# A hybrid layer's FFN in two phases: second phase's operands in small steps, first weight block earlier, last group by column halves

## The chip, the cores and the metric

The kernel runs on one core of a Trainium2 chip. The metric is the device time of one execution in microseconds; the median of three runs of the kernel before is 2200.96 us (2199.82 to 2202.98). The engines are named as in the profile: PE multiplies matrices, PEld loads its weights, DVE, ACT and POOL work on elements, SP issues every DMA of this kernel in one ordered queue.

## The reference

One layer of a two-mixer trunk over 2048 positions and 1024 channels, all in float32: an S5 state-space mixer and an mLSTM mixer, joined by an output projection, then a feed-forward part (FFN) with a squared ReLU, and a last norm:

```
x = x + concat(S5, mLSTM) @ W_out
h = rmsnorm(x, norm_ffn_g)
x = x + square(relu(h @ W1)) @ W2        # 1024 -> 4096 -> 1024
return rmsnorm(x, final_norm_g)
```

The mixers are not touched by the change.

## The kernel before

**Layout.** Channels lie on the 128 partitions, positions along the free axis; a tile of 512 positions is a token block. Blocks 0 and 1 make the FFN's first phase, blocks 2 and 3 its second. Every large product is made of float16 high and low parts, three matmuls for one (L1300, L1301, L1302 in the FFN).

**Stages in time.** The mixers take the span to about 735 us, then come the gated unit of S5 (to 800), the output projection of blocks 0 and 1 (to 840), that of blocks 2 and 3 in alternation (to 935), FFN phase 1 of 2 (935 to about 1600), phase 2 (to 2176), and the last norm with the stores (to 2199.5).

**The FFN.** Both of its products go by a seven-product scheme on 2 x 2 blocks (Strassen-Winograd), so the operands are not the plain blocks but sums and differences of them, each split into a high and a low part. `f1_stream` runs over 16 units of W1 in each phase. A unit is seven products in two half steps each, and its results, after the ReLU and square, become seven pairs B11, B21, T2, T1, T3, B22, T4 in the tag "hd", a ring of 22 buffers of 2 KB per partition. `f2_stream` runs over 8 groups of W2 per phase, a group being four row pairs (mp) of seven products of 512 columns; each product is added to the accumulator `accx` by a DVE operation at L1399. The main loop takes one half step of F1 and one product of F2 in turn, F2 behind by LAG = 34.

**Operands of F1.** `hprep(ph, k, rb)` makes one quarter k of the seven operands: four norms on DVE (L1129, multiply by a gain and by the row factor `rb`, which lies in PSUM), four subtractions in `combos` (L1085 to L1094), seven splits (L1079: ACT copies the high part, L1080: POOL or DVE subtracts it, POOL in five of seven). For phase 1 the operands go into resident tiles `hop`. For phase 2 the block's x comes from a DRAM buffer `x2d` (L1128) into hd buffers, and each pair is stored to the DRAM buffer `hopd` (L1115), to be loaded when phase 2 begins. These four calls stand at i = 2, 6, 10 and 14 of the main loop, the first half steps of phase 1.

**Weights.** Each raw block of 1 MB is loaded (`w1_load` L1160, `w2_load` L1209), reduced to its largest value (L1148), scaled and split (L1178 ACT, L1179 DVE); POOL makes the weight sums (L1192, L1232 to L1235). `w2_load` has a single buffer, "stg"; W1's raw blocks alternate between "w0" and "w1". The first block of W1 is loaded, scaled and prepared between m = 3 and m = 5 of the output projection of blocks 2 and 3, beside `hprep(0, ...)`.

**Ends.** `final0` writes the output of phase 1 while phase 2 runs: for each of 16 tiles a load from the DRAM buffer `x2f`, a norm on DVE (L1439) and a store, every fourth i, all through the one buffer of tag "tb". `final1` does the same for phase 2 at the very end: row sums, row factors, then 10 multiplies on DVE (L1458), 6 on ACT and POOL (L1455, L1456), 8 stores of 512 KB (L1460).

**Order.** A scheduler at build time puts the instructions of each engine in a fixed order by its own cost estimates; on the chip each engine runs its list in that order and waits where an operand is late. SP does so too, so a DMA that waits for its buffer holds every DMA behind it.

## Time and profile before

| what | value |
|---|---|
| median of three runs | 2200.96 us |
| profiled execution, its time | 2201.49 us |
| its span | 2199.5 us |
| PE busy | 2045.9 us, 93% |
| DVE busy | 1702.6 us, 77% |
| ACT, POOL busy | 48%, 51% |

The profiled execution lies 0.5 us above the median, and its span leaves 2.0 us of its time outside. A row of a table by stretches gives start and end in us, the stretch's length, then for each engine its busy time in it with the number of instructions, the mean granted clock of PE (1 is 2.4 GHz, 0.5 is 1.2 GHz), the share of time that the DMA engines were busy and what they moved in GB/s. A busy PE is no PE at its peak, so the number of matmuls in a stretch says more than the busy time.

### The profile page before, as it was taken

What the parts mean: (1) busy time and instruction counts of PE and PEld (TensorE: products, weight loads), DVE (VectorE), ACT (ScalarE), POOL (GpSimd) and SP (SyncE); (2) the same over time, 40 slices, a digit from 0 to 9 for tenths busy, and PEclk for the clock granted to TensorE, in tenths of its full rate; (3) what the DMA queues carried; (4) which work ended last, traced back from release to release, by engine and by line L of the source; (5) the groups of instructions that cost most, each with busy time, mean ns of one, the idle gap of its engine ahead of it and who ended that gap; (6) DMA issues with size and microseconds to landing.
All of it is one profiled execution on the core that took longest, in us unless ns stands there. A gap on an engine that the chain in (4) does not pass through costs nothing.

```text
span 2199.5 us, 29564 instructions
## 1 busy us (share of the span) xinstructions
PE 2045.9 (93%) x11021; PEld 1148.6 (52%) x11021; DVE 1702.6 (77%) x2829; ACT 1055.5 (48%) x1879; POOL 1125.3 (51%) x1095
## 2 busy tenths in 40 slices
PE   6999899899998799867999999999999899999996
PEld 4987767676776344333444444444444344444442
DVE  7878888887867544978988888878887786777776
ACT  5426455555544222345545454545564354545443
POOL 2135566564223201567665655565684566557454
PEclk9999999999999899988999999999999999999998
DMA  5111111211103212343111111115332321111102
GB/s 174 60 52 57 50 44 30 82 34 54 63 20 134 87 39 71 116 149 125 58 58 58 58 58 58 58 58 191 134 134 101 134 72 58 58 48 68 39 20 96
DMA packets 53551, 168.14 MB, mean 76 GB/s; under 512 B 7776, under 2 KB 17184, under 8 KB 40864
## 3 DMA queue, kind: packets, MB, share of 16 engines
q1 hardware_dynamic: 53408, 166.26, 22.5%
q8 instruction: 86, 1.41, 0.3%
q14 instruction: 57, 0.47, 0.1%
HBM read 129.44 MB, written 28.41 MB: 72 GB/s over the span
## 4 chain that ended last, share of the span: by engine, by line
PE 56%; DVE 22%; DMA 7%; POOL 5%; ACT 3%; issue 3%; SPq 1%; POOLq 0%; DVEq 0%; ACTq 0%
PE gx L1300 4%; PE gx L1302 4%; PE gx L1301 4%; PE fx L1300 4%; PE fx L1301 4%; PE fx L1302 4%; PE gv L1300 2%; PE gv L1302 2%; PE gv L1301 2%; PE fv L1302 2%; PE fv L1300 2%; PE fv L1301 2%; PE po L157 2%; PE po L158 2%; PE po L159 2%
## 5 line engine op out<-in xcount | busy, mean ns | idle before, releaser
L1178 ACT ACTIVATE w2o<-r,fs_b 128x512 f16<-128x512 f32 (+1 forms) x128 | 105.4, 824 | 153.3 <-PE gx L1302 76.3
L1329 ACT ACTIVATE e<-e 128x512 f32<-128x512 f32 x96 | 60.3, 628 | 211.0 <-DVE e L1369 93.0
L1301 PEld LDWEIGHTS <-w2o 128*128 128x128 f16 x896 | 87.7, 98 | 128.3 <-issue 27.3
L1179 DVE SCALAR_TENSOR_TENSOR w2o<-r,fs_b,w2o 128x512 f16<-128x512 f32 (+1 forms) x128 | 132.9, 1039 | 25.7 <-ACT w2o L1178 25.4
L1300 PEld LDWEIGHTS <-w2o 128*128 128x128 f16 x896 | 87.8, 98 | 108.9 <-issue 3.0
L1302 PEld LDWEIGHTS <-w2o 128*128 128x128 f16 x896 | 87.7, 98 | 106.5 <-DVE w2o L1179 1.4
L159 PE MATMUL pv<-w_vo,xn 128*128 128x256 f16 x512 | 142.0, 277 | 0.2 <-DVE xn L443 0.2
L157 PE MATMUL pv<-w_vo,xn 128*128 128x256 f16 x512 | 142.2, 278 | 0.0
L158 PE MATMUL pv<-w_vo,xn 128*128 128x256 f16 x512 | 142.0, 277 | 0.0
L1235 POOL TENSOR_TENSOR r<-r,s 128x256 f32<-128x256 f32 x64 | 63.6, 994 | 134.2 <-DVE w2o L1179 131.5
L1399 DVE SCALAR_TENSOR_TENSOR x2b<-gx,dd,x2b 128x512 f32<-128x512 f32 x128 | 94.7, 744 | 38.5 <-PE gx L1302 38.5
L1399 DVE SCALAR_TENSOR_TENSOR x<-gx,dd,x 128x512 f32<-128x512 f32 x128 | 94.7, 743 | 14.7 <-PE gx L1302 14.5
L1300 PE MATMUL fx<-hop,wB 128*128 128x512 f16 x256 | 97.7, 382 | 8.2 <-ACT e L1358 6.7
L157 PE MATMUL pq<-xn,w_qk 128*128 128x512 f16 x256 | 98.1, 384 | 0.0
L158 PE MATMUL pq<-xn,w_qk 128*128 128x512 f16 x256 | 98.1, 383 | 0.0
L159 PE MATMUL pq<-xn,w_qk 128*128 128x512 f16 x256 | 97.8, 382 | 0.0
L1301 PE MATMUL fx<-hop,wB 128*128 128x512 f16 x256 | 97.8, 382 | 0.0
L1302 PE MATMUL fx<-hop,wB 128*128 128x512 f16 x256 | 97.7, 382 | 0.0
L158 PEld LDWEIGHTS <-xn 128*128 128x128 f16 x768 | 88.2, 115 | 9.8 <-issue 0.6
L157 PEld LDWEIGHTS <-xn 128*128 128x128 f16 x768 | 88.1, 115 | 9.8 <-ACT xn L442 0.2
L159 PEld LDWEIGHTS <-xn 128*128 128x128 f16 x768 | 87.9, 115 | 9.1 <-DVE xn L443 1.6
L1192 POOL TENSOR_TENSOR s<-r 128x512 f32<-128x512 f32 x32 | 55.3, 1728 | 72.0 <-issue 70.3
(1319 smaller groups left out, 6861.8 us busy)
## 6 DMA issues: line engine op xcount, KB each, us to landing
r<-in_w_dram SPq DMA_DIRECT2D x64, 1024.0 KB, 4.9
xt<-in_xN_dram SPq DMA_DIRECT2D x16, 512.0 KB, 4.6
rt<-rh SPq DMA_DIRECT2D x64, 128.0 KB, 2.3
hopd<-ho SPq DMA_DIRECT2D x28, 256.0 KB, 2.5
hop<-hopd SPq DMA_DIRECT2D x7, 1024.0 KB, 4.7
st_vo<-in_wvo_dram SPq DMA_DIRECT2D x4, 1024.0 KB, 5.1
st_qk<-in_wqk_dram SPq DMA_DIRECT2D x4, 1024.0 KB, 5.0
bcm<-negM_d SPq DMA_DIRECT2D x16, 256.0 KB, 3.1
```

The source lines that it names most:

```text
L157: T.matmul(out, wh, xh, start=(i == 0), stop=False)
L158: T.matmul(out, wh, xl, start=False, stop=False)
L159: T.matmul(out, wl, xh, start=False, stop=(i == n - 1))
L1178: S.activation(out=hi, in_=src, func=AF.Copy, scale=sg)
L1179: V.scalar_tensor_tensor(out=lo, in0=src, scalar=sg, in1=hi, op0=ALU.mult, op1=ALU.subtract)
L1192: G.tensor_tensor(out=s12[:, 0], in0=raw[:, 2], in1=raw[:, 3], op=ALU.add)
L1235: G.tensor_tensor(out=r[:, 1], in0=r[:, 1], in1=s12[:, 1], op=ALU.subtract)
L1300: T.matmul(out, wh, xh, start=(first and i == 0), stop=False, skip_group_check=True)
L1301: T.matmul(out, wh, xl, start=False, stop=False, skip_group_check=True)
L1302: T.matmul(out, wl, xh, start=False, stop=(last and i == n - 1), skip_group_check=True)
L1329: S.activation(out=x, in_=x if src is None else src, func=AF.Relu, scale=scale)
L1399: V.scalar_tensor_tensor(out=acc[:, j, c, :], in0=bk[b], scalar=dd, in1=acc[:, j, c, :], op0=ALU.mult, op1=ALU.add)
```

## The change

**Operands of the second phase.** `hprep(1, ...)` becomes a generator, `hprep1`, of 68 small steps, one at every second i from HP1 = 46, so over 136 products' worth of phase 1. Its norms read the row factor from a copy in SBUF (`rsh`, made once by ACT) where those of before read PSUM. All its splits have the subtraction on POOL. Its tiles stay in the ring hd, which has 23 buffers now.

**First weight block.** The first block of W1 is loaded, scaled and prepared beside the output projection of block 1, in the buffer "stg", and `hprep(0, ...)` moves up to m = 1, 2, 4, 5.

**Between the phases.** The accumulators of phase 2 are loaded right behind the store of those of phase 1, and `final0` has ring buffers and loads one tile ahead.

**Last group.** `f2_last` computes the last four products' rows of F2 in two halves of 256 columns, first all of one half, then all of the other. The row factors, multiplies and stores of the first half stand beside the matmuls of the second; there are 16 stores of 256 KB. The last two weight blocks are prepared into "w0" and "w1" and need no buffer of the ones before.

```diff
-NHD = 22
+HP1 = 46
+HB = 256
+NHD = 23
...
-            else:
-                hd = fp.tile([P, 2, TB], F16, name=f"ho{i}{k}", tag="hd", bufs=NHD)
-                split(hd[:, 0, :], hd[:, 1, :], src, E)
-                nc.sync.dma_start(out=hopd[i][:, :, k, :], in_=hd)
...
+    def hprep1(rs):
...
+        for k in range(4):
...
+            def norm(t_, kk, c):
+                V.scalar_tensor_tensor(out=t_, in0=t_, scalar=ct[:, O_GFFN + kk:O_GFFN + kk + 1], in1=rs[c], op0=ALU.mult, op1=ALU.mult)
...
+                ho = fp.tile([P, 2, TB], F16, name=f"ho{i}{k}", tag="hd", bufs=NHD)
+                split(ho[:, 0, :], ho[:, 1, :], src, G)
+                nc.sync.dma_start(out=hopd[i][:, :, k, :], in_=ho)
...
+            b12 = load(k, 1)
+            b22 = load(k + 4, 1)
+            yield
+            norm(b12, k, 1)
+            yield
+            norm(b22, k + 4, 1)
+            yield
+            t3 = hd_("t3")
+            sub(t3, b22, b12)
+            b11 = load(k, 0)
+            yield
+            put("T3", t3)
+            yield
...
+            put("T1", b12)
+            yield
+            sub(b22, b22, b12)
...
+        if tag is None:
+            wp, tag = ((wpool, "w2"), (r3, "wo3"))[j]
...
-    for m in range(KD):
-        out_proj(1, m)
     hop[0:2] = [None, None]
...
     xo = gl["msp"].tile([P, 8, TB], F32, name="xo", tag="ms0")
+    psx["a"] = psl, "ml"
+    for m in range(KD):
+        out_proj(1, m)
+        if m == 0:
+            w1_load(0, 0, stg, "stg")
+        if m == 1:
+            rb0[0] = rms_rows(psum_colsum([accs[0]], TB, psl, "ml", "f0"), 4, ones_h, psl, "ml", "f0")
+        if m == 3:
+            w1_scale(0, 0)
+        if m in (4, 5, 6):
+            w1_prep(0, 0, m - 4)
     for m in range(KD):
...
-        if m == 3:
-            w1_load(0, 0)
-            psx["a"] = psl, "ml"
...
+        if m == 0:
+            rb0[1] = rms_rows(psum_colsum([accs[1]], TB, psl, "ml", "f1"), 4, ones_h, psl, "ml", "f1")
+        elif m in (1, 2, 4, 5):
+            hprep(0, (None, 0, 1, None, 2, 3)[m], rb0)
         if m == 4:
...
-        if m == 5:
+        if m == 7:
             w1_scale(0, 1)
-            w1_prep(0, 0, 2)
         out_proj(3, m)
...
-        if ph == 1 and g == 0:
-            accx[mp] = accxp.tile([P, 2, 2, TB], F32, name=f"x2b{mp}", tag=f"ax{mp}")
-            nc.sync.dma_start(out=accx[mp].rearrange("p m c t -> p m (c t)"), in_=x2d[:, 2 * mp:2 * mp + 2, :])
...
+            nc.sync.dma_start(out=x2f[:, 2 * mp:2 * mp + 2, :], in_=acc.rearrange("p m c t -> p m (c t)"))
+            accx[mp] = accxp.tile([P, 2, 2, TB], F32, name=f"x2b{mp}", tag=f"ax{mp}")
+            nc.sync.dma_start(out=accx[mp].rearrange("p m c t -> p m (c t)"), in_=x2d[:, 2 * mp:2 * mp + 2, :])
...
-            for g in range(NFB // 2):
+            for g in range(NFB // 2 - ph):
                 for mp in range(4):
                     yield from f2_mp(ph, g, mp, "g")
+        yield from f2_last()
...
+        xs_ = {}
+        for n in range(2 * KD + 1):
+            if n < 2 * KD:
+                xs_[n] = fp.tile([P, TB], F32, name=f"of{n}", tag="hd", bufs=NHD)
+                nc.sync.dma_start(out=xs_[n], in_=x2f[:, n // 2, (n % 2) * TB:(n % 2 + 1) * TB])
+            if n >= 1:
+                m, c = (n - 1) // 2, (n - 1) % 2
+                xt_ = xs_.pop(n - 1)
                 V.scalar_tensor_tensor(out=xt_, in0=xt_, scalar=ct[:, O_GFIN + m:O_GFIN + m + 1], in1=rs[c], op0=ALU.mult, op1=ALU.mult)
                 nc.sync.dma_start(out=out_v[:, m, c * TB:(c + 1) * TB], in_=xt_)
-                yield
-
-    def final1():
-        rbs = []
-        for c in range(2):
-            ss = psum_colsum([accf[c]], TB, psf, "gx", f"o1{c}", 2)
...
+    def f2_last():
...
+        g = NFB // 2 - 1
+        for s in range(2):
+            ts = slice(s * HB, (s + 1) * HB)
...
+            for mp in range(4):
...
+                for i, (b, wn, op) in enumerate(PR2):
...
+                    mmx(bk[b][:, 0:HB], [(w[wn][:, 0, f * P:(f + 1) * P], w[wn][:, 1, f * P:(f + 1) * P], hid[1, 2 * g + f, op][:, 0, ts], hid[1, 2 * g + f, op][:, 1, ts]) for f in range(2)], first=(i in (0, 1, 5)), last=True)
+                    j, c = ((0, 0), (1, 1), (0, 1), (0, 1), (1, 1), (0, 0), (1, 0))[i]
+                    V.scalar_tensor_tensor(out=acc[:, j, c, ts], in0=bk[b][:, 0:HB], scalar=dd, in1=acc[:, j, c, ts], op0=ALU.mult, op1=ALU.add)
+                    if s == 0 and i == 0 and qd + 1 < 32:
+                        w2_prep(1, qd + 1, *(((wpool, "w0"), (wpool, "w1"))[mp - 1] if mp in (1, 2) else (None, None)))
+                    if s == 0 and i == 1 and qd % 2 == 0 and qd // 2 + 1 < 16:
...
+                for c in range(2):
+                    for j in range(2):
...
+            rs = tb(f"rs1{s}", "acc", 2)
+            S.copy(rs, rb)
             for m in range(KD):
-                x_ = accx[m // 2][:, m % 2, c, :]
-                g = ct[:, O_GFIN + m:O_GFIN + m + 1]
...
+                x_ = accx[m // 2][:, m % 2, :, ts]
+                g_ = ct[:, O_GFIN + m:O_GFIN + m + 1]
+                if s == 0 or m in (1, 4, 7):
+                    S.activation(out=x_, in_=x_, func=AF.Copy, scale=g_)
+                    G.tensor_tensor(out=x_, in0=x_, in1=rs.rearrange("p (c t) -> p c t", c=2), op=ALU.mult)
                 else:
-                    V.scalar_tensor_tensor(out=x_, in0=x_, scalar=g, in1=rbs[c], op0=ALU.mult, op1=ALU.mult)
-                if m % 2 == 1:
-                    nc.sync.dma_start(out=out_v[:, m - 1:m + 1, 2 * TB + c * TB:2 * TB + (c + 1) * TB], in_=accx[m // 2][:, :, c, :])
+                    V.scalar_tensor_tensor(out=x_, in0=x_, scalar=g_, in1=rb.rearrange("p (c t) -> p c t", c=2), op0=ALU.mult, op1=ALU.mult)
+                nc.sync.dma_start(out=out_v[:, m].rearrange("p (h c t) -> p h c t", h=2, c=2)[:, 1, :, ts], in_=x_)
+                if s == 0 and m % 2 == 1:
+                    yield
 
...
-    rb1 = [rms_rows(psum_colsum([accs[t]], TB, psf, "gx", f"f{t}", 2), 4, ones_h, psf, "g" + "wv"[t - 2], f"f{t}", 1) for t in (2, 3)]
...
+    for t in (2, 3):
+        rb = rms_rows(psum_colsum([accs[t]], TB, psf, "gx", f"f{t}", 2), 4, ones_h, psf, "g" + "wv"[t - 2], f"f{t}", 1)
+        r_ = r3.tile([P, TB], F32, name=f"rsh{t}", tag="acc", bufs=2)
+        S.copy(r_, rb)
+        rs1.append(r_)
+    hp1 = hprep1(rs1)
...
-        if i in (2, 6, 10, 14):
-            hprep(1, (i - 2) // 4, rb1)
+        if i >= HP1 and (i - HP1) % 2 == 0:
+            next(hp1, None)
...
-    final1()
```

The places below show the order of instructions by engine, a line of the kernel, the operation, its output and inputs with buffer numbers, and the shape. On DVE, in the first steps of phase 1, the kernel before has the norms and subtractions of the second phase's last quarter (b30 to b71, t3h, ho) among the ReLU's operations of F1's unit 1 (e101, e201).

```order
L1369 SCALAR_TENSOR_TENSOR e101_10123<-fv01_10125,qf1_9490,e101_10123 128x512
L1094 TENSOR_TENSOR t2f00_9956<-b2100_9973,t2f00_9956 128x512
L1129 SCALAR_TENSOR_TENSOR b30_1_9993<-b30_1_9993,ct_70,rb_f2_9674 128x512
L1129 SCALAR_TENSOR_TENSOR b71_1_9996<-b71_1_9996,ct_70,rb_f3_9686 128x512
L1129 SCALAR_TENSOR_TENSOR b31_1_9999<-b31_1_9999,ct_70,rb_f3_9686 128x512
L1365 SCALAR_TENSOR_TENSOR e201_10138<-fx01_9986,qf1_9490,e201_10138 128x512
L1129 SCALAR_TENSOR_TENSOR b70_1_10002<-b70_1_10002,ct_70,rb_f2_9674 128x512
L1080 TENSOR_TENSOR ho53_10009<-b71_1_9996,ho53_10009 128x512
```

At the same place the changed kernel has accumulations of F2 (x2), weight splits (wB, wA, wC) and the ReLU's operations of unit 2 (e002).

```order
L1447 SCALAR_TENSOR_TENSOR x2_1_8142<-gx01_10288,dd0_9888,x2_1_8142 128x512
L1227 SCALAR_TENSOR_TENSOR wB02_10044<-r1_02_9705,fs_a2_9737,wB02_10044 128x1536
L1400 SCALAR_TENSOR_TENSOR e002_10062<-fw02_10064,qf2_9919,e002_10062 128x512
L1096 TENSOR_TENSOR t2f01_10017<-b2101_10034,t2f01_10017 128x512
L1227 SCALAR_TENSOR_TENSOR wA03_10095<-r1_03_9865,fs_a3_9912,wA03_10095 128x1024
L1447 SCALAR_TENSOR_TENSOR x2_0_8140<-gv00_10155,dd0_9888,x2_0_8140 128x512
```

None of the second phase's operand work is left among them. On SP, in the middle of phase 1, the kernel before issues nothing but the raw weight blocks of W2 (r2) and W1 (r1) in alternation.

```order
L1209 DMA r2_04_11274<-in_w2_dram 128x2048
L1160 DMA r1_08_11440<-in_w1_dram 128x2048
L1209 DMA r2_05_11579<-in_w2_dram 128x2048
L1160 DMA r1_09_11745<-in_w1_dram 128x2048
L1209 DMA r2_06_11892<-in_w2_dram 128x2048
```

In the changed kernel loads of x (b) and stores of operand pairs (hopd) stand between the same weight blocks.

```order
L1257 DMA r2_05_11467<-in_w2_dram 128x2048
L1143 DMA hopd3_8136<-ho31_11510 256x1x512
L1208 DMA r1_09_11646<-in_w1_dram 128x2048
L1257 DMA r2_06_11802<-in_w2_dram 128x2048
L1143 DMA hopd2_8135<-ho21_11628 256x1x512
L1208 DMA r1_010_11978<-in_w1_dram 128x2048
L1143 DMA hopd1_8134<-ho11_11664 256x1x512
L1133 DMA b21_2_11810<-x2d_8131 128x512
L1133 DMA b61_2_11812<-x2d_8131 128x512
L1143 DMA hopd6_8139<-ho61_11759 256x1x512
```

So 18 weight blocks stand between the first load of x and the last store of an operand. On DVE, near the end, the kernel before splits the weights of the last two row pairs (w2o130, w2o131) between the accumulations (x2b) of 512 columns.

```order
L1179 SCALAR_TENSOR_TENSOR w2o130_19214<-r2_115_19158,fs_b15_14739,w2o130_19214 128x768
L1399 SCALAR_TENSOR_TENSOR x2b2_15522<-gv130_19302,dd15_14742,x2b2_15522 128x512
L1399 SCALAR_TENSOR_TENSOR x2b1_15386<-gx129_19206,dd14_14447,x2b1_15386 128x512
L1179 SCALAR_TENSOR_TENSOR w2o131_19290<-r2_115_19158,fs_b15_14739,w2o131_19290 128x512
L1399 SCALAR_TENSOR_TENSOR x2b2_15522<-gx130_19282,dd15_14742,x2b2_15522 128x512
L1179 SCALAR_TENSOR_TENSOR w2o131_19290<-s2_131_19293,fs_b15_14739,w2o131_19290 128x512
L1399 SCALAR_TENSOR_TENSOR x2b2_15522<-gv130_19302,dd15_14742,x2b2_15522 128x512
L1179 SCALAR_TENSOR_TENSOR w2o131_19290<-r2_115_19158,fs_b15_14739,w2o131_19290 128x768
```

In the changed kernel the last of these splits stand among the accumulations of the first half (gx1300, gx1310, 256 columns), and the second half (gx1281) begins behind all of them.

```order
L1512 SCALAR_TENSOR_TENSOR x2b3_15227<-gw1310_19393,dd15_14742,x2b3_15227 128x256
L1227 SCALAR_TENSOR_TENSOR w2o130_19212<-r2_115_19158,fs_b15_14739,w2o130_19212 128x768
L1512 SCALAR_TENSOR_TENSOR x2b3_15227<-gx1310_19356,dd15_14742,x2b3_15227 128x256
L1227 SCALAR_TENSOR_TENSOR w2o131_19288<-r2_115_19158,fs_b15_14739,w2o131_19288 128x768
L1023 TENSOR_TENSOR af000_19196<-af000_19196,sq_o0300_19408 128x256
L1512 SCALAR_TENSOR_TENSOR x2b2_15083<-gv1300_19300,dd15_14742,x2b2_15083 128x256
...
L1512 SCALAR_TENSOR_TENSOR x2b0_14775<-gx1281_19462,dd14_14447,x2b0_14775 128x256
L1512 SCALAR_TENSOR_TENSOR x2b0_14775<-gw1281_19499,dd14_14447,x2b0_14775 128x256
```

The first half of all four row pairs has moved ahead of the second half of any.

## Rows read from the trace of the kernel before

**Rows 1.** Busy time by engine in stretches of the FFN.

```profile
964.00:1020.00 56.00, 28.14 (x89) 10.54 (x88) 44.38 (x57) 31.64 (x51) 37.60 (x28) 0.73 0.52 171
1020.00:1120.00 100.00, 96.75 (x445) 43.33 (x444) 90.66 (x125) 53.64 (x79) 69.77 (x60) 1.00 0.19 66
1120.00:1640.00 520.00, 520.00 (x2434) 240.64 (x2433) 434.48 (x605) 274.67 (x401) 320.55 (x277) 1.00 0.25 88
1640.00:1800.00 160.00, 143.19 (x647) 63.84 (x646) 120.09 (x137) 71.35 (x104) 90.84 (x76) 0.99 0.31 106
1800.00:2140.00 340.00, 339.85 (x1575) 154.00 (x1574) 250.51 (x283) 172.56 (x251) 199.06 (x170) 1.00 0.15 50
```

**Rows 2.** What PE waited for, 964 to 1020 us (total, times, longest).

```profile
PE fv L1300 <- ACT e L1361: 11.1, 1, 11.1
PE fx L1300 <- ACT e L1358: 6.7, 1, 6.7
```

**Rows 3.** 935 to 1020 us, DVE, ACT, POOL on tiles ho, then tiles b.

```profile
935.00:1020.00 85.00, 8.96 (x8) 17.36 (x28) 29.65 (x20) 0.82 0.46 149
...
935.00:1020.00 85.00, 39.66 (x41) 12.93 (x22) 12.55 (x9) 0.82 0.46 149
```

**Rows 4.** Norms by line, min/median/max ns: second phase's operands, first phase's outputs.

```profile
L1129 DVE SCALAR_TENSOR_TENSOR b<-b,ct,rb_f x16: 735/747/749, 942.1 to 1007.4; 128x512 f32<-128x512 f32 x16
...
L1439 DVE SCALAR_TENSOR_TENSOR of<-of,ct,rs x16: 751/947/1785, 1661.9 to 1766.3; 128x512 f32<-128x512 f32 x16
```

**Rows 5.** What DVE waited for, 1120 to 1482 us.

```profile
DVE x L1399 <- PE gv L1302: 17.3, 15, 1.9
DVE x L1399 <- PE gx L1302: 9.8, 11, 2.7
DVE m_b L1148 <- DMA r<-in_w_dram: 9.7, 10, 1.1
```

**Rows 6.** What the DMA queue on SP waited for, 1120 to 1482 us.

```profile
SPq L1209 <- DVE w2o L1179: 219.6, 10, 22.6
SPq L1160 <- DVE wB L1179: 139.2, 10, 14.5
```

**Rows 7.** Waits of DVE and PE, 1640 to 1800 us, and the chain of waits there.

```profile
DVE of L1439 <- DMA of<-x2f: 21.2, 10, 4.8
...
PE gx L1300 <- DVE x2b L1399: 11.7, 11, 2.3
...
1694.76 2.01 DMA out_dram<-of
1696.78 2.70 DMA of<-x2f
```

**Rows 8.** The tail by engine, in order of time: start, duration in us.

```profile
2141.97 0.72 ACT L1178 ACTIVATE w2o<-r,fs_b 128x512 f16<-128x512 f32 x1 [1.67 <-PE gx L1302]
...
2146.76 4.83 DMA r<-in_w_dram
...
2163.09 0.73 POOL L1235 TENSOR_TENSOR r<-r,s 128x256 f32<-128x256 f32 x1 [3.15 <-DVE w2o L1179]
...
2164.95 1.37 DVE L1179 SCALAR_TENSOR_TENSOR w2o<-r,fs_b,w2o 128x768 f16<-128x768 f32 x1
...
2175.51 0.38 PE L1302 MATMUL gx<-hd115T,w2o 128*128 128x512 f16 x1
...
2184.70 7.41 POOL L1456 TENSOR_TENSOR x2b<-x2b,rs 128x512 f32<-128x512 f32 x6 [1.66 <-ACT rs L1450]
```

**Rows 9.** Matmuls of 256 columns on PE, first and last of 13 in a line.

```profile
306.19 0.27 PE L159 MATMUL pv<-w_vo,xn 128*128 128x256 f16 x1
...
307.50 0.27 PE L159 MATMUL pv<-w_vo,xn 128*128 128x256 f16 x1
```

**Rows 10.** SP and DVE in the gated unit's stretch, 740 to 746 us.

```profile
742.22 0.33 SPq L1209 DMA_DIRECT2D r<-in_w_dram  x1
...
744.70 0.75 DVE L779 SCALAR_TENSOR_TENSOR gth<-pgl,zd,bg 128x512 f32<-128x512 f32 x1 [1.27 <-PE pgl L159]
```

More of the change, by code (lines that the diff above doesn't have):

```diff
@@ L983, in trunk, with tb @@
     accx = [None] * 4
-    def tb(name, tag="tb"):
-        return r3.tile([P, TB], F32, name=name, tag=tag)
+    def tb(name, tag="tb", bufs=1):
+        return r3.tile([P, TB], F32, name=name, tag=tag, bufs=bufs)
     x2d = drp.tile([P, KD, 2 * TB], F32, name="x2d")
@@ L1133, in hprep, with hd_, load, put @@
         put("B21", b[1, 0])
-        combos(b[0, 0], b[0, 1], b[1, 0], b[1, 1], put, V, f"h{ph}{k}", tp)
+        combos(b[0, 0], b[0, 1], b[1, 0], b[1, 1], put, V, f"h{ph}{k}", tb)
+    def hprep1(rs):
+        for k in range(4):
+            def hd_(name):
+                return fp.tile([P, TB], F32, name=f"{name}_{k}", tag="hd", bufs=NHD)
+            def load(kk, c):
+                t_ = hd_(f"b{kk}{c}")
+                nc.sync.dma_start(out=t_, in_=x2d[:, kk, c * TB:(c + 1) * TB])
+                return t_
+            def norm(t_, kk, c):
+                V.scalar_tensor_tensor(out=t_, in0=t_, scalar=ct[:, O_GFFN + kk:O_GFFN + kk + 1], in1=rs[c], op0=ALU.mult, op1=ALU.mult)
+            def put(op, src):
+                i = OPS.index(op)
+                ho = fp.tile([P, 2, TB], F16, name=f"ho{i}{k}", tag="hd", bufs=NHD)
+                split(ho[:, 0, :], ho[:, 1, :], src, G)
+                nc.sync.dma_start(out=hopd[i][:, :, k, :], in_=ho)
+            def sub(o, x, y):
+                V.tensor_tensor(out=o, in0=x, in1=y, op=ALU.subtract)
+            b12 = load(k, 1)
[11 more added lines that the diff above has]
+            yield
+            norm(b11, k, 0)
+            yield
+            put("B22", b22)
+            yield
+            put("B11", b11)
+            yield
+            sub(b12, b12, b11)
+            b21 = load(k + 4, 0)
+            yield
+            put("T1", b12)
+            yield
+            sub(b22, b22, b12)
+            yield
+            norm(b21, k + 4, 0)
+            put("T2", b22)
+            yield
+            put("B21", b21)
+            yield
+            sub(b22, b21, b22)
+            yield
+            put("T4", b22)
+            yield
     raw1, sg1, mp1, wops1 = {}, {}, {}, {}
@@ L1156, in f_scale, with w1_load @@
         return mp, sg
-    def w1_load(ph, u):
-        raw = raw1[ph, u] = wpool.tile([P, 4, 512], F32, name=f"r1_{ph}{u}", tag=f"w{u % 2}")
+    def w1_load(ph, u, wp=None, tag=None):
+        raw = raw1[ph, u] = (wp or wpool).tile([P, 4, 512], F32, name=f"r1_{ph}{u}", tag=tag or f"w{u % 2}")
         nc.sync.dma_start(out=raw, in_=w1[u])
@@ L1407, in f2_mp @@
             yield
-        if g == NFB // 2 - 1:
+        if ph == 0 and g == NFB // 2 - 1:
             for c in range(2):
```

65 lines of the change are left out of this document (28 added, 37 removed).

## The prediction

> **What bounds the kernel now.** I read the table by stretches first, because one mean over the span hides the places that matter. In the long middle stretches PE sets the pace: 1575 matmuls in 340 us, 0.216 us each, with PE busy all the time [rows 1]. Matmuls that are missing at this pace tell what a stretch loses. From 964 to 1020 there is room for 56/0.216 = 259, and 89 were run: 170 x 0.216 = 36.7 us lost. From 1020 to 1120 it is 463 against 445, 3.9 us lost; from 1640 to 1800 it is 741 against 647, 20.3 us lost. Then PE's waits say who was late. In the first stretch it stands 11.1 and 6.7 us for results that ACT had still to scale [rows 2], since ACT, DVE and POOL are at the same time busy with the second phase's operands. In the third it waits for accumulations on DVE, and DVE in turn waits 21.2 us for the tiles of `final0` to come back from DRAM [rows 7]. So three places can pay: the start of phase 1, the passage between the phases, and the end behind the last matmul.
>
> **The operands of the second phase leave the start.** In 935 to 1020 they cost ACT 17.4 and POOL 29.7 us for the splits, and DVE 9.0 us of them [rows 3]. The tiles b hold 41 DVE instructions of 39.7 us: 16 norms of 0.747 [rows 4] are 12.0, the 8 splits' subtractions 9.0, and 17 others 18.7, of which the 16 subtractions are 17.6. So DVE is relieved of 12.0 + 9.0 + 17.6 = 38.6 us of work in stretches that are 40.6 us (36.7 + 3.9) short. That the two are nearly equal is the ground for taking most of it as gain. What stays late is F1's own start: its first results pass ACT, POOL and DVE before F2 can use them. I leave 7 us for it (2 to 15). **Gain 34 us (26 to 39).**
>
> **They come into the middle of phase 1.** A product's step is 12 matmuls, 12 x 0.216 = 2.59 us; 68 steps at every second one are 136 x 2.59 = 352 us. DVE does 434 us of work in 520 there [rows 1], 84%, and part of the rest is free only in name. What I count as free is where DVE waits for F2's products: 17.3 + 9.8 = 27.1 us in 362 [rows 5], so 26.4 in 352. Added are 17.6 us of subtractions, 16 norms, and waits for the loads of x.
>
> The norms are of a form that this use does not show: they now take both tile inputs from SBUF. The nearest row is the norm of `final0`, with the same form, 0.751 to 1.785 us, median 0.947, where the one with an input in PSUM takes 0.735 to 0.749 [rows 4]. I take 0.95: 15.2 us (12.0 to 28.6). The Trainium skill, "SBUF — State Buffer", section "Who interferes with whom", says that DVE's second port pair is shared with GpSimd under an exclusive lock, which is why a norm with two SBUF inputs should stand behind POOL's work; the spread up to 1.785 us agrees. By that rule the old placing of the row factor in PSUM would be 16 x 0.2 = 3.2 us cheaper, and the sum would end 3 us lower.
>
> For the loads I take 3 us of waiting (0, as they are issued one or two steps ahead, to a whole landing of a quarter-megabyte tile, 2.70 us [rows 7], for half of the 16, 22). So DVE is short by 17.6 + 15.2 + 3 - 26.4 = 9.4, about **10 us lost (0 to 34)**; the low end is that idle time spent in other waits takes the work in, the upper that norms are at their longest with half the loads late, 17.6 + 28.6 + 22 - 26.4 = 42, less a fifth for norms and late loads that fall together. POOL gets 28 splits of about 1.48 us (29.65/20 [rows 3]), 41 us in 352, on top of 62% [rows 1]: 74%. ACT gets 17.4 on 53%. Neither becomes the bound.
>
> **Between the phases.** Through one buffer each tile of `final0` is a ring of store and load, 2.01 + 2.70 us in the chain [rows 7], which DVE waits for with everything queued behind it, PE's accumulations too (11.7 us). With ring buffers and a load one tile ahead the chain is cut for most tiles. By the order of the changed kernel 5 of 16 loads still reuse the buffer of an `of` tile just before them and stay serial. 11 of 16 of 20.3 is 14; the earlier load of the accumulators lets me take **17 us gained (8 to 20)**.
>
> **First weight block and output projection.** Its work moves some 60 us ahead beside a PE that was not waiting for it, and 13 DVE operations of `hprep(0)` now stand between the evictions of block 2. I cost it at **0 (-4 to +5)**: the cover is DVE's free time beside these matmuls. One reduction moves ahead by much more: that of the first block of W1 stands on DVE before the gated unit's operation at 744.70, and its load takes the place in the SP queue that was issued at 742.22 [rows 10]. A load of that size takes 4.83 us [rows 8]: landing 747.05, so DVE and the gated unit are held for 2.4 us. **2 us lost (0 to 5).**
>
> **The end.** In the trace the splits of row pair 29 start at 2141.97, as they wait for a product of pair 28's start [rows 8]; the changed kernel's are one product ahead, 2139.4. The last raw block is loaded when they end: 4.8 us later, 4.83 us long [rows 8], so it lands at 2149.0. Both last pairs' weights took from 2151.59 to 2166.32 (2164.95 + 1.37), 14.7 us, of which 3.15 us is POOL's wait for a buffer that the change no longer shares [rows 8]: 11.5, so 2160.6, and the first half of columns ends some 2 us later, at 2162.6. The second half is 168 matmuls of 256 columns, (307.50 - 306.19)/12 = 0.109 us each [rows 9], 6 of them beside the first half: 162 x 0.109 = 17.7, so 2180.3. Before, the last matmul began at 2175.51 [rows 8], so PE ends 4.4 us later than before (0.38 for its own length). Behind it 23.6 us were left of the span. Half of the multiplies go: POOL's 7.41 for six [rows 8] become 3.7, and there is one row factor in the place of two; I take 5 us off, 18.6. End: 2198.9 against 2199.5. **0.6 us gained, taken as 0 (9 gained to 7 lost).** The low end is an earlier last load by one more product and stores that are half as long; the upper is two more products of waiting for weights.
>
> There PE stands idle for several us before the second half. In this trace the clock fell where PE stood: the granted clock was 0.73 from 964 to 1020 [rows 1], a mix of 2.4 and 1.2 GHz, and it was 1.00 where PE was busy. If the first 5 us of the second half run at 1.2 GHz they give 2.5 us away. The Trainium skill, "TensorE: Matmul & The Clock Gate", section "HAM oscillation — how this bites in real kernels", tells the same of waits for loads between bursts of matmuls; by it the sum would be 2.5 us higher, which my upper end holds.
>
> **Sum.** 2201.5 - 34 + 10 - 17 + 2 + 0 + 0 = 2162.5. The profiled execution lies 0.5 us above the median, so 2162 us, 39 us or 1.8% faster.
>
> **Rivals.**
> *DVE saturates.* A wait for F2's product is not free time if the next product's accumulation is wanted at once: then all 38.6 us that DVE gains in the middle are lost to PE, 28 more than in my sum, about 2190. For it: DVE is at 84% with many ordered hand-overs. Against: the accumulations have two buffers (gx) to run behind in. Chance 0.13.
> *The start is F1's own.* If ACT's lateness at 964 to 1020 comes from the first units' chain and not from the operands, only some 15 of 34 us come back: 2181. For it: the longest wait is for an ACT scaling of F1 itself. Against: nearly the same sums, above. Chance 0.08.
> *The change doesn't do what it says in the passage or the tail:* the ring's buffers come free so late that loads stay serial (5 gained in the place of 17, 2174), or weights come so late that the halves cost 10 us (2172). Chance 0.10.
> *Slower: the queue on SP.* Its DMAs are ordered, and it is blocked nearly always: 219.6 + 139.2 of 362 us [rows 6]. Each store of a pair waits for POOL's subtraction and each load of x for a ring buffer, and 18 weight blocks stand behind them. The raw blocks of W2 have one buffer, and DVE already waits 9.7 us in 10 times for them to land [rows 5]: a later issue is a later reduction, with all of DVE behind it. Ten such blocks lie in this stretch. If each is issued one step pair late, 2 x 2.59 = 5.2 us, that is 52 us: 2162 + 52 = 2214. It decides from 39/10 = 3.9 us a block. Against: POOL has a quarter of its time free, and its subtraction is usually done within its own step. Chance 0.08.
>
> **How the numbers follow.** My sum has 0.61, between its own ends of about 2150 and 2178. The range 2145 to 2190 takes in the start and passage rivals and half of the first: 0.61 less a little for the tails, + 0.18 + 0.07, above 0.8. What a measurement of this kernel can tell from no change is about 0.2%, 4.4 us. Faster holds my sum, both partial rivals and most of the saturated case, 0.88; half of the queue's chance, if it takes only 39 us, and the worst of the saturated case make 0.04 for the same; 0.08 is left for slower.
>
> **What would show it.** Right: PE's count from 964 to 1120 near 680 and no long wait for ACT there; DVE above 90% from 1055 to 1400, with waits for F2's products nearly gone and PE some 10 us short; PE above 700 matmuls in the 160 us at the passage, with no more than a third of the 21 us of waiting for `of`; the last matmul 3 to 7 us later against the start of the last group, and some 18 us behind it. Wrong: PE waiting for x2 accumulations all through the spread steps (the first rival); the reductions of W2's blocks waiting 3 us or more for their landing (the queue); PE still below 0.9 busy behind 964.

## The result and the profile after

The changed kernel takes 2183.18 us (median of four runs, 2180.98 to 2186.09), against 2200.93 of the kernel before measured beside it: 0.9915 of its time, 95% interval 0.9904 to 0.9927. That is 18 us or 0.85% faster. Forecast were 39 us and a range of 2145 to 2190: the sign and the range hold, the size is less than half. The profiled execution's span is 2180.9 us, 18.6 less than before. The stretches that answer to [rows 1], with the same columns:

```profile
964.00:1020.00 56.00, 54.31 (x254) 24.86 (x252) 48.33 (x63) 36.68 (x55) 44.13 (x34) 1.00 0.22 77
1020.00:1120.00 100.00, 92.17 (x418) 41.32 (x417) 89.71 (x126) 46.35 (x69) 61.40 (x48) 0.98 0.22 73
1120.00:1640.00 520.00, 501.77 (x2320) 228.86 (x2319) 449.27 (x594) 276.25 (x408) 349.22 (x293) 1.00 0.30 103
1640.00:1800.00 160.00, 159.35 (x741) 72.63 (x740) 129.63 (x148) 83.22 (x118) 99.77 (x81) 1.00 0.30 101
```

The start has 254 matmuls where it had 89, the passage 741 where it had 647: both holes are closed. The long middle stretch has 2320 where it had 2434: a new, shallow hole.

Stretches of fixed time mix places of the program, so I took the time of one event in both traces, the first matmul of each unit of F1. Two of them before, and the same two after:

```profile
1080.68 0.38 PE L1300 MATMUL fx<-hop,wA 128*128 128x512 f16 x1
...
1449.18 0.38 PE L1300 MATMUL fx<-hop,wA 128*128 128x512 f16 x1
```

```profile
1041.59 0.38 PE L1351 MATMUL fx<-hop,wA 128*128 128x512 f16 x1
...
1443.52 0.38 PE L1351 MATMUL fx<-hop,wA 128*128 128x512 f16 x1
```

These are units 4 and 14 of phase 1; the others are read in the same way:

| event | before, us | after, us | after less before |
|---|---|---|---|
| F1 begins | 935.46 | 935.85 | +0.4 |
| unit 4 | 1080.68 | 1041.59 | -39.1 |
| unit 14 | 1449.18 | 1443.52 | -5.7 |
| phase 2, unit 3 | 1634.39 | 1628.79 | -5.6 |
| phase 2, unit 7 | 1800.87 | 1775.80 | -25.1 |
| last matmul of F1 | 2126.01 | 2101.53 | -24.5 |
| end of the span | 2199.5 | 2180.9 | -18.6 |

So 39.5 us are gained at the start, 33.4 given back between units 4 and 14 where the operands' steps now lie, 19.4 gained in the passage, 5.9 lost behind F1's end. Of the 20 us by which the change falls short of the forecast 23 come from the steps and 6 from the end; the start, the passage and the first weight block together came out some 9 better.

**The steps.** The ten units in one row each, before and after, with the columns of [rows 1]:

```profile
1080.68:1449.18 368.50, 367.60 (x1721) 170.30 (x1720) 317.85 (x466) 187.11 (x271) 218.22 (x193) 1.00 0.17 58
...
1041.59:1443.52 401.93, 376.35 (x1721) 170.17 (x1720) 361.20 (x492) 201.24 (x300) 270.22 (x225) 0.99 0.24 81
```

The same 1721 matmuls take 33 us more. PE hardly waited before; now it waits all through for accumulations on DVE:

```profile
PE gx L1300 <- DVE x L1399: 0.7, 2, 0.5
...
PE gx L1351 <- DVE x L1447: 13.6, 13, 2.7
PE gv L1351 <- DVE x L1447: 7.2, 6, 2.3
```

Twice in these units the granted clock fell for a short time from 2.4 to 1.2 GHz, right behind waits of 2.38 and 2.25 us. The second of them, and the stretch around it:

```profile
1154.95 0.38 PE L1351 MATMUL gv<-hd04B,w2o 128*128 128x512 f16 x1 [2.25 <-DVE x L1447]
...
1151.59:1161.59 10.00, 7.75 (x29) 3.06 (x27) 9.04 (x11) 2.34 (x4) 7.38 (x6) 0.83 0.31 103
```

By the mean of 0.99 over the ten units that is at most 0.01 x 402, some 4 us of PE's time. The kernel with the last group at full width, below, has one such fall here and the same loss of 33.4, so it is not shown that it cost anything.

DVE's waits there, before and after:

```profile
DVE x L1399 <- PE gv L1302: 16.9, 14, 1.6
DVE m_b L1148 <- DMA r<-in_w_dram: 9.7, 10, 1.2
DVE x L1399 <- PE gx L1302: 5.1, 8, 1.0
```

```profile
DVE m_b L1196 <- DMA r<-in_w_dram: 18.0, 10, 4.3
DVE x L1447 <- PE gv L1353: 6.0, 6, 1.3
DVE w2o L1227 <- ACT w2o L1226: 5.2, 7, 1.5
```

Time in which DVE waited for products has been used, as forecast, but DVE now waits nearly twice as long for W2's raw blocks. And DVE's operations by form, first after (two lines of the steps, one of W1's split), then before, where the split's row has a mean of 1833 ns:

```profile
L1227 DVE SCALAR_TENSOR_TENSOR wB<-r,fs_a,wB 128x1536 f16<-128x1536 f32 x10 | 23.8, 2376 | 0.0
L1137 DVE SCALAR_TENSOR_TENSOR b<-b,ct,rsh 128x512 f32<-128x512 f32 x15 | 18.2, 1231 | 0.0
L1146 DVE TENSOR_TENSOR b<-b,b 128x512 f32<-128x512 f32 x12 | 15.5, 1291 | 3.2 <-POOL ho L1082 3.2
```

```profile
L1179 DVE SCALAR_TENSOR_TENSOR wB<-r,fs_a,wB 128x1536 f16<-128x1536 f32 x10 | 18.3, 1833 | 0.4
```

**The passage.** The norm of `final0`, with the total of its waits below it, answers to [rows 4, 7]: 21.2 us of waiting became 1.8.

```profile
L1493 DVE SCALAR_TENSOR_TENSOR of<-of,ct,rs x16: 739/1277/1649, 1669.5 to 1826.0; 128x512 f32<-128x512 f32 x16
...
its engine sat idle before it (us, times) until:
  DMA of<-x2f: 1.8, 1
```

**The end**, which answers to [rows 8]: the splits of row pair 29, the last raw block's load, PE's longest wait, the last split, PE's last matmul.

```profile
2115.24 0.72 ACT L1226 ACTIVATE w2o<-r,fs_b 128x512 f16<-128x512 f32 x1 [0.70 <-PE gx L1353]
...
2120.20 0.33 SPq L1257 DMA_DIRECT2D r<-in_w_dram  x1
...
2125.82 0.28 PE L1351 MATMUL gx<-hd114B,w2o 128*128 128x256 f16 x1 [1.94 <-ACT w2o L1226]
...
2134.78 1.00 DVE L1227 SCALAR_TENSOR_TENSOR w2o<-r,fs_b,w2o 128x768 f16<-128x768 f32 x1
...
2160.91 0.27 PE L1353 MATMUL gx<-hd115T,w2o 128*128 128x256 f16 x1
```

### The profile page after: what moved, and what is told of

Same layout as the page of the kernel before. It is cut to its first block, busy times and chain, and to the rows that moved or that the text cites. A ratio compares the mean times of both kernels' runs of the same rounds, so it can differ in the third digit from the quotient of the medians.

```text
span 2180.9 us, 30020 instructions
## 1 busy us (share of the span) xinstructions
PE 2042.0 (94%) x11205; PEld 1162.8 (53%) x11205; DVE 1711.0 (78%) x2850; ACT 1062.5 (49%) x1902; POOL 1150.6 (53%) x1112
## 4 chain that ended last, share of the span: by engine, by line
PE 48%; DVE 26%; POOL 7%; DMA 5%; issue 5%; ACT 4%; SPq 1%; POOLq 0%; DVEq 0%; ACTq 0%
DVE w2o L1227 3%; PE gx L1351 3%; PE gx L1352 3%; PE gx L1353 3%; PE fx L1351 3%; PE fx L1352 3%; PE fx L1353 3%; DMA r<-in_w_dram 3%; DVE x L1447 2%; PE po L159 2%; PE po L160 2%; PE po L161 2%; DVE y L247 2%; PE fv L1351 1%; PE fv L1352 1%
## 5 line engine op out<-in xcount | busy, mean ns | idle before, releaser
L1226 ACT ACTIVATE w2o<-r,fs_b 128x768 f16<-128x768 f32 (+1 forms) x128 | 105.4, 824 | 135.3 <-POOL r L1284 60.2
L1352 PEld LDWEIGHTS <-w2o 128*128 128x128 f16 x952 | 93.3, 98 | 131.8 <-issue 36.5
L1227 DVE SCALAR_TENSOR_TENSOR w2o<-r,fs_b,w2o 128x768 f16<-128x768 f32 (+1 forms) x128 | 134.7, 1053 | 25.1 <-ACT w2o L1226 24.3
L1353 PEld LDWEIGHTS <-w2o 128*128 128x128 f16 x952 | 93.1, 98 | 103.9 <-DVE w2o L1227 3.2
L1351 PEld LDWEIGHTS <-w2o 128*128 128x128 f16 x952 | 93.5, 98 | 103.0 <-ACT w2o L1226 3.1
L1447 DVE SCALAR_TENSOR_TENSOR x2b<-gx,dd,x2b 128x512 f32<-128x512 f32 x112 | 82.7, 744 | 53.1 <-PE gx L1353 53.0
L1447 DVE SCALAR_TENSOR_TENSOR x<-gx,dd,x 128x512 f32<-128x512 f32 x128 | 94.2, 741 | 10.7 <-PE gx L1353 10.5
```

The lines of the kernel that those rows point to most:

```text
L1226: S.activation(out=hi, in_=src, func=AF.Copy, scale=sg)
L1227: V.scalar_tensor_tensor(out=lo, in0=src, scalar=sg, in1=hi, op0=ALU.mult, op1=ALU.subtract)
L1351: T.matmul(out, wh, xh, start=(first and i == 0), stop=False, skip_group_check=True)
L1352: T.matmul(out, wh, xl, start=False, stop=False, skip_group_check=True)
L1353: T.matmul(out, wl, xh, start=False, stop=(last and i == n - 1), skip_group_check=True)
L1447: V.scalar_tensor_tensor(out=acc[:, j, c, :], in0=bk[b], scalar=dd, in1=acc[:, j, c, :], op0=ALU.mult, op1=ALU.add)
```

## The experiments

Times are medians; the kernel before, run beside each group, had 2200.9 to 2202.6. "Loss" is what units 4 to 14 take above the 368.5 us of the kernel before; for the changed kernel it is 33.4.

**Three undo one part of the change.** The operands back at the front:

```
-        if i >= HP1 and (i - HP1) % 2 == 0:
-            next(hp1, None)
+        if i in (2, 6, 10, 14):
+            for _ in range(17):
+                next(hp1, None)
```

> The changed kernel with the same 68 steps run in four bursts of 17 at i = 2, 6, 10, 14, where the kernel before had them; all else as changed. If the operands are what held the start, the 39 us of the start are lost again and the 33 us of the spread come back: about 2189 (2184 to 2196). If the earlier first weight block alone freed the start, it stays free and only the 33 us come back: 2150 to 2160.

2203.8 us. Unit 4 begins 52.9 us later than in the changed kernel, at 1094.48, and the ten units take 367.8: no loss. The operands held the start, though all else is as changed; the earlier weight block alone does not free it. The time lies above the range: unit 4 comes 13.8 us later than in the kernel before too (1080.68), and no run shows why.

`final0` with one buffer again:

```
-                xs_[n] = fp.tile([P, TB], F32, name=f"of{n}", tag="hd", bufs=NHD)
+                xt_ = tb(f"of{m}{c}")
```

> The changed kernel with final0 as before: one buffer, each load behind the store before it. If the ring buffers and the load ahead made the 19 us of the passage, they are lost: 2202 (2198 to 2205). If the earlier load of the accumulators made them, 2183 to 2190.

2202.7 us, and DVE's wait is back:

```profile
DVE of L1489 <- DMA of<-x2f: 20.3, 9, 3.6
```

From unit 3 to unit 7 of phase 2 it takes 166.0 us, the kernel before 166.5, the changed one 147.0: the ring buffers and the load ahead make all of the 19 us, the earlier load of the accumulators next to nothing.

The last group at full width, as before:

```
-        yield from f2_last()
...
+    final1()
```

> The changed kernel with the last group and the final norm as in the kernel before (512 columns, final1 behind all matmuls, two preparation buffers). From F1's last matmul to the end of the span the kernel before took 73.5 us, the changed one 79.4: 5.9 us less, 2177 (2174 to 2180). If the halves pay and the 5.9 us come from something else: 2183 or more.

2177.2 us (0.9885, 0.987 to 0.990): the halves of columns cost 6 us.

**Four move or leave out the steps' work,** to tell DVE's time from the queue on SP. Norms and subtractions left out:

```
-                V.scalar_tensor_tensor(out=t_, in0=t_, scalar=ct[:, O_GFFN + kk:O_GFFN + kk + 1], in1=rs[c], op0=ALU.mult, op1=ALU.mult)
+                pass
...
-                V.tensor_tensor(out=o, in0=x, in1=y, op=ALU.subtract)
+                pass
```

> The changed kernel (2183.2 us) with the 16 norms and 16 subtractions of the second phase's operands left out of the spread steps (the splits then take the plain loaded x, so what is computed is not the reference); loads, splits and stores of the operands stay. Unit starts of F1 show that the spread steps cost 33.4 us between units 4 and 14. Theory D (DVE is short of time: 43 us more work there, only some 10 us less idle): the loss falls to 0 to 8 us, time 2150 to 2158. Theory Q (the operand DMAs hold up the weight blocks in the ordered queue on SP): the DMAs are all there, loss stays above 25, time 2175 to 2185.

2159.9 us, loss 9.8: nearly D's range, far from Q's. (The edit also leaves out the four ring tiles `t3`.) Subtractions on POOL, then norms too, ACT scaling and POOL multiplying:

```
-                V.tensor_tensor(out=o, in0=x, in1=y, op=ALU.subtract)
+                G.tensor_tensor(out=o, in0=x, in1=y, op=ALU.subtract)
...
+                S.activation(out=t_, in_=t_, func=AF.Copy, scale=ct[:, O_GFFN + kk:O_GFFN + kk + 1])
+                G.tensor_tensor(out=t_, in0=t_, in1=rs[c], op=ALU.mult)
```

> The changed kernel with the 16 subtractions of the spread steps on POOL in the place of DVE. 15.5 + 4.3 = 19.8 us leave DVE, 16 x about 1.2 = 19 us come to POOL (270 busy of 402 us there). Theory D: loss 33 falls by 15 to 22, time 2161 to 2168. Theory Q: no change, 2180 to 2186. Theory P (POOL's share of the common SBUF port, or POOL itself, is what is short): no gain or a loss, 2183 to 2195.

> The changed kernel with norms and subtractions of the spread steps off DVE: the norm is an ACT scaling (about 0.7 us) and a POOL multiply by the row factor, the subtraction is on POOL. 38 us leave DVE, some 38 come to POOL and 11 to ACT. Theory D: loss falls to 0 to 8, time 2150 to 2158. Theory Q: 2180 to 2186. Theory P: POOL at 270 + 38 of 370 us gets late itself, time 2165 to 2190.

2186.8 and 2187.9 us, loss 36.1 and 39.2: within P's ranges, outside D's. Loads and stores on ACT's queue:

```
-                nc.sync.dma_start(out=t_, in_=x2d[:, kk, c * TB:(c + 1) * TB])
+                nc.scalar.dma_start(out=t_, in_=x2d[:, kk, c * TB:(c + 1) * TB])
...
-                nc.sync.dma_start(out=hopd[i][:, :, k, :], in_=ho)
+                nc.scalar.dma_start(out=hopd[i][:, :, k, :], in_=ho)
```

> The changed kernel with the 16 loads of x and 28 stores of operand pairs issued from ACT's queue, so that only weight blocks and hop loads stand in SP's. DVE's work is unchanged. Theory Q: most of the 33 us come back, 2150 to 2160. Theory D: at most the 8 us come back by which DVE waits longer for W2's blocks than before (18.0 against 9.7 us), time 2174 to 2185.

2188.0 us, loss 36.1. In this run the DMAs stand in ACT's list instead, which could cost as much as it saves; but in the run with the work left out all of them are still on SP, and the loss is 9.8. So Q falls. D, in the form that DVE's busy time alone counts, falls too, since 38 us moved away bring nothing. The ten units of the run with all on POOL, and its longest wait on DVE:

```profile
1040.86:1448.53 407.67, 376.95 (x1721) 170.20 (x1720) 342.31 (x460) 210.72 (x315) 315.84 (x256) 0.99 0.24 80
```

```profile
DVE w2o L1228 <- ACT w2o L1227: 26.7, 14, 5.0
```

POOL is busy 316 of 408 us, DVE still 342 (318 before, for the same work of its own). DVE stands for weight splits whose high part ACT had not made yet, and ACT in turn for POOL's weight sums; the second wait, in the kernel before, in the changed kernel, where it has grown already, and in this run:

```profile
ACT w2o L1178 <- POOL r L1235: 6.2, 7, 1.1
...
ACT w2o L1226 <- POOL r L1284: 21.0, 12, 7.1
...
ACT w2o L1227 <- POOL r L1285: 21.8, 13, 3.5
```

**Spacing, POOL, the ring.** The low half as a second ACT copy; then, in another kernel, a step every third i:

```
-                split(ho[:, 0, :], ho[:, 1, :], src, G)
+                S.activation(out=ho[:, 0, :], in_=src, func=AF.Copy)
+                S.activation(out=ho[:, 1, :], in_=src, func=AF.Copy)
```

```
+HP1 = 10
...
+        if i >= HP1 and (i - HP1) % 3 == 0:
```

> The changed kernel with DVE's 16 norms and 16 subtractions in the spread steps, but the low half of each of the 28 operand pairs is a second ACT copy in the place of POOL's subtraction (the low halves are then wrong, so what is computed is not the reference). POOL is relieved of about 41 us, ACT gets 28 x 0.6 = 17 more. Theory D (DVE's own time): only the 5 us go by which DVE's other operations got longer, loss between units 4 and 14 of 26 to 33, time 2176 to 2184. Theory S (a step's work is handed between DVE, ACT and POOL in order, so work on any of them delays the weight chain): loss 10 to 22, time 2160 to 2172.

> The changed kernel with the 68 steps from i = 10 at every third i (204 i's in the place of 136). If each unit of phase 1 has a fixed room of about 1 us on DVE, loss = 43 us of work less 1 us for each of 14.5 units against 9.7: 28 in the place of 33, time 2176 to 2180. If the loss comes from bunching (several operations in one step push the weight splits back), it falls to 10 to 18, time 2158 to 2170. If the first steps, that now lie in the start, hurt as they did before, the start gives back 5 to 10: up to 2190.

2181.0 us, loss 29.1; and 2183.0 us, the same as changed, with a loss of 27.7 in the ten units and 2.7 us more in front of them. POOL's 41 us of subtractions carry at most 4 of the 33: the time can't be told from that of the changed kernel, and the granted clock stayed at 1.00 in the ten units here. So P is not the whole of it, S, which asked for a loss of 10 to 22, falls in this form, and so does bunching. A second raw buffer for W2 needs room, so the ring falls to 19 in both of these, and the first has both edits:

```
+NHD = 19
...
+        raw = raw2[ph, v] = (stg if v % 2 == 0 else fp).tile([P, 2, 4, 256], F32, name=f"r2_{ph}{v}", tag="stg")
```

> The changed kernel with a second buffer for W2's raw blocks (odd blocks in the FFN's own pool; to make room the ring hd has 19 buffers, not 23). In the spread steps DVE is idle 40.7 us of 402, 18.0 of them for W2's blocks to land. If late landing is what keeps DVE's last idle time from use, the loss of 33 falls by 10 to 18 against the same ring without the second buffer (next kernel). If DVE is simply full, by less than 5.

> The changed kernel with 19 ring buffers in the place of 23 and nothing else, to read the kernel with a second W2 buffer against. If the ring were short in the spread steps already, the loss grows, 2190 or more; if not, 2181 to 2186.

2181.2 and 2210.9 us; in the ten units a loss of 24.7 with the second buffer and of 43.8 without it. The shorter ring alone adds 10 us there. The second buffer takes off 19, more than was expected, and with it DVE's wait for W2's blocks is gone, which with the shorter ring alone is

```profile
DVE m_b L1196 <- DMA r<-in_w_dram: 16.2, 8, 4.3
```

So with this ring late landing of W2's blocks is a good part of the loss. In total the second buffer is worth 30 us where the ring is short, but both edits together stand where the changed kernel stands: 8.7 us better in the ten units, and slower behind them. A ring of more than 23 was not run. To have a second buffer with the full ring, the raw block was loaded, reduced and scaled in halves:

```
+            raw2["p"] = stg.tile([P, 2, 4, 256], F32, name="r2_p", tag="stg")
+        raw = raw2[ph, v] = raw2["p"][:, v % 2]
+        nc.sync.dma_start(out=raw, in_=w2[v // 2][:, v % 2])
```

> The changed kernel with W2's raw block loaded, reduced and scaled in two halves of 512 KB (one for each row pair), each half loaded as soon as the preparation before has freed it, so a raw half waits a whole row pair (18 us) before it is needed. DVE's work grows by some 1.5 us a unit (small scale operations). Theory R (W2's single raw buffer is what the spread steps make late): loss of 33 falls to 5 to 15 and the wait in the last group goes, 2150 to 2165. Theory D (DVE full): loss stays or grows, 2178 to 2195.

> The kernel before with W2's raw block in halves and nothing else. PE does not wait there in the middle of phase 1, so theory R gives no gain but for the last group's 3 us: 2195 to 2202. Theory D: the extra small operations fit in DVE's idle time, 2198 to 2205.

2196.6 and 2216.5 us: 13 and 14 us slower than the kernels they come from, with losses of 63.1 (behind a start 16.5 us earlier) and 12.6. The edit also doubles the small scale operations, so it is no clean test of R: in the kernel before, DVE's waits for ACT grow from 4.4 to 27.3 us in the ten units. With full width it was 2188.6 (by R 2150 to 2162), and with every third step besides 2196.7, 8 us slower where the same or up to 8 faster was forecast. As a remedy it fails.

**Is DVE full?** DVE operations alone added to the kernel before, and DVE work taken from the changed kernel outside the steps (W1's and W2's reductions):

```
+        if 46 <= i < 174 and i % 4 == 2:
+            V.tensor_tensor(out=du, in0=accx[((i - 35) // 7) % 4][:, 0, 0, :], in1=accs[2], op=ALU.subtract)
```

```
-            mp, sg2[v] = f_scale(raw.rearrange("p m s n -> p (m s n)"), f"b{v}")
+            mp, sg2[v] = f_scale(raw.rearrange("p m s n -> p (m s n)")[:, 0:256], f"b{v}")
```

> The kernel before with 32 more DVE subtractions (128 x 512, both inputs in SBUF, result not used), one at every fourth i from 46 to 170, each reading an accumulator tile so that it stays in its place. About 32 x 1.15 = 37 us of DVE work, no POOL, ACT or DMA work. If DVE is full at 86% busy, PE loses 0.7 to 0.8 of it: 26 to 29 us, 2220 to 2232. If the 27 us in which DVE waits for F2's products are free time, as predicted, 10 us or less: 2201 to 2212.

> The changed kernel with the reductions to the largest weight (32 in phase 1, 2.28 us each) taken over 256 of 2048 columns only, so the scales come from part of each block. In units 4 to 14 some 38 us leave DVE, all operand steps stay. DVE full: the 33 us fall to 0 to 8, 2148 to 2158. Loss of the operand steps themselves (order, rings, POOL): at most 10 come back, 2172 to 2183.

2214.0 us, between the two ranges, of which 5.5 us are late by unit 4 already and 8.5 are lost in the ten units; and 2179.8, loss 25.5. The added operations, in the first run's ten units, and what W2's landing then costs:

```profile
L1478 DVE TENSOR_TENSOR du<-x,acc 128x512 f32<-128x512 f32 x30 | 29.0, 965 | 0.8
```

```profile
DVE m_b L1148 <- DMA r<-in_w_dram: 23.6, 10, 2.9
```

29 us of DVE work cost 8.5: most of the 26 us in which DVE waited for products was free. And in the second run DVE is busy for 319.7 us, no more than before the change, yet the loss is 25.5:

```profile
1039.96:1433.95 393.99, 373.81 (x1721) 170.36 (x1720) 319.73 (x493) 202.92 (x300) 267.28 (x219) 0.99 0.25 83
```

The waits of DVE in the ten units, added up by what ended them:

| kernel | length | DVE busy | for PE | for DMA | for ACT | for POOL | POOL busy |
|---|---|---|---|---|---|---|---|
| before | 368.5 | 317.9 | 25.8 | 10.7 | 4.4 | 5.5 | 218 |
| changed | 401.9 | 361.2 | 6.0 | 18.7 | 7.1 | 7.2 | 270 |
| no norms, subtractions | 378.3 | 325.2 | 7.7 | 23.0 | 17.0 | 3.0 | 262 |
| both on POOL | 407.7 | 342.3 | 2.0 | 13.2 | 38.9 | 9.3 | 316 |
| low halves by ACT | 397.6 | 354.4 | 2.4 | 27.7 | 8.6 | 2.8 | 228 |
| 32 operations added to before | 377.0 | 339.7 | 4.6 | 26.4 | 0 | 2.1 | 228 |
| light reductions | 394.0 | 319.7 | 19.2 | 17.1 | 23.7 | 11.6 | 267 |

What is taken from one engine comes back for the most part as waiting for another; only leaving out the steps' own norms and subtractions brought most of the loss back.

One rival stands beside all of these runs. The scheduler orders every engine's list anew for each kernel. Compared by operation and tile in the traces, at most these DVE operations of the ten units stand in the order of the changed kernel: 391 of 461 without norms and subtractions, 364 of 459 with both on POOL, 402 of 491 with the low halves by ACT, 385 of 492 with the light reductions (with the last group at full width all 491). So each of them changes the order together with the work, and none tells one from the other.

**The best version.** Full width and every third step together:

> The changed kernel with the last group at full width and the steps at every third i from 10, the two edits that did not lose. Tail 5.9 us less than as changed, spread at most 3 us less: 2174 to 2178, against 2177.2 for the first edit alone.

2175.0 us (0.9881, 0.9866 to 0.9895), 26 us faster than before and 8 faster than the change. From full width alone (0.9885) it can't be told apart.

## Why the prediction was right and wrong

- **The start, forecast 34 gained (26 to 39):** 39.5. The argument that the missing matmuls and the operands' work were nearly equal held; the 7 us that I left for F1's own chain were not needed. The rival that gave only 15 is refuted by the time itself, and the run with the operands at the front shows that they were what held the start.
- **The steps, forecast 10 lost (0 to 34): this step failed.** Measured 33.4. By the table, from before to changed: DVE's busy time +43.3, its waits for PE -19.8, for DMA, ACT and POOL +12.4, and the gaps that belong to no wait -2.5. Forecast were 32.8 of work and 3 of waits for loads, less 26.4 usable. So the work was mis-sized by 10.5: the norms took 1.23 us where 0.95 was taken (3.0 in all), the subtractions 1.24 where 1.10 was (2.2), and DVE's other operations together got 5.3 us longer, though there were six fewer of them. (Added up one by one, W1's and W2's splits took some 15 us longer, W1's largest 2376 ns in place of 1833; DVE's operations overlap a little, 392 us added up against 361 busy, so such sums exceed the busy time.) The usable time came out somewhat smaller: 19.8 were used of the 26.4, and the 32 added operations used 21. What had no term at all were the hand-overs: W2's blocks late by another 8 us, waits for ACT and POOL. Together that is 10.5 + 9.4 of waits beyond the 3 + 6.6 of idle time not used - 2.5 = 24, from the 9.4 of the sum to 33.4. The Trainium skill, "SBUF — State Buffer", section "Who interferes with whom", has DVE and GpSimd share a port pair under a lock; the longer norms agree: the two of the 16 that lay beside no operation of POOL took 0.74 us, the eight that took over 1 us all lay beside one. In the sum I had taken the median of the row.
- **Which resource it is** the runs narrow but don't settle. Leaving out the steps' norms and subtractions gives 24 of 33 back; taking the same time from DVE elsewhere gives 8; moving it to POOL none; a second buffer for W2's blocks 19 of 44 where the ring is short. So it is more than DVE's time: the steps' operations are handed from DVE to ACT to POOL, each running its list in order, and weight splits queue behind them. The chain of work that ended last agrees. Before, it lies on PE for 348 of the 368 us of the ten units; in the changed kernel on DVE for 214, POOL 58, loads of weight blocks 37, PE 27, ACT 24 of 402:

```profile
by line: DVE x L1447 11.2%; issue 10.5%; DMA r<-in_w_dram 10.4%; DVE w2o L1227 9.7%; DVE m_b L1196 4.0%; DVE m_a L1196 3.9%; DVE b L1137 3.3%; DVE wB L1227 3.1%; DVE wA L1227 2.8%; POOL ho L1082 2.7%; DVE t2f L1096 2.6%; DVE b L1146 1.6%; D
```

  It is one of several paths of nearly the same length: with the last group at full width, whose order here is the same, it has 156 us on DVE and 126 on PE. That the hand-overs are the cause is argued from the waits. No run changed their order alone, and every run that changed the work changed the order too, so it stays open.
- **The rival "DVE saturates"** gave 2190 and had about the right size, with half its reason: PE did wait for accumulations all through the steps, its sign, but DVE's waits for products could be used. Its 38.6 us still hold the 9.0 of splits that the change gives to POOL; with the sum's own 32.8 it would have been 2185.
- **The rival "queue on SP"**, 3.9 us a block to break even: W2's ten blocks were waited for 18.0 us in place of 9.7, 0.8 us each, and the queue's relief changed nothing. Wrong here.
- **The passage, 17 (8 to 20):** 19.4, all of it by the buffers. The 3 us added for the earlier load of the accumulators came true for another reason: that 5 of 16 loads share a buffer cost hardly anything, 1.8 us of waiting.
- **The first weight block, 2 lost:** DVE did wait for it in the gated unit, 3.91 us where 2.4 were worked out, but F1 began only 0.4 us late: work behind covered it.

```profile
746.68 2.29 DVE L1196 TENSOR_REDUCE m_a<-r 128x1 f32<-128x2048 f32 x1 [3.91 <-DMA r<-in_w_dram]
```

- **The end, 0 (-9 to +7):** 5.9 lost. Counted from F1's last matmul, the last split ended at 34.3 us where the sum has 34.6 (2160.6 - 2126.0). But PE ended at 59.7 where it has 54.3: it took 25.4 us from that split on, not 19.7. The pace of the short matmuls was as forecast, 0.109 us; 190 of them were left, 10 more than the sum has, 20.7 us in all. What had no term are the 20 matmuls that make the row sums and row factors and now stand between the products, some 3.5 us, and 1.1 us of waits for DVE:

```profile
L1527 PE MATMUL ss_o<-one,af 128*128 128x1 f32 x18 | 2.3, 241 | 0.5 <-DVE af L1023 0.5
...
L1061 PE MATMUL rb_o<-dg_o,one 128*128 128x512 f32 x2 | 1.0, 594 | 0.0
...
PE gx L1351 <- DVE x2b L1512: 0.6, 1, 0.6
```

  The granted clock was 1.00 there from 2120 to 2150, behind a longest wait of 1.94 us; the 2.5 us that it might have cost were not lost. Behind the last matmul 19.7 us were left where 18.6 were taken.

Of the signs named ahead, PE's count in the start (254 + 418 = 672) and the waiting for `of` pointed right. The tail did so in part: 19.7 us behind the last matmul, but that came 9.8 us later against the start of the last group (54.2 us behind it in place of 44.5), not 3 to 7. DVE at 90% with PE 10 us short pointed to the failure: DVE was at 90%, and PE 33 short. Of the signs of being wrong, PE waiting for accumulations came true.

## What to carry to other kernels

Work moved into a stretch where PE is busy all the time is not paid by the free time of one engine alone: add the waits that it brings to every engine that it is handed through. Here the loss came out at the upper end of the range, where the engine's idle time was mostly hand-overs. To find out whether an engine is full, add work to it alone, and take work from it elsewhere; the two together tell more than moving it. Where a scheduler makes the order, compare the order of the lists too, before a difference is put down to the work. A tail that splits a group to overlap its end must be priced with everything that comes to stand between the products, here the matmuls of the norm.
